# The last stage's normalizing factor: one root per token and a second product, or the root of a broadcast row

## The chip, the cores and the metric

The kernel runs on one core of a Trainium2 chip. A core has five engines with a queue of instructions each: TensorE (PE in the profile) multiplies matrices, with its weight loads shown apart (PEld); VectorE (DVE) and ScalarE (ACT) work elementwise; GpSimd (POOL) works elementwise too, on SBUF alone; SyncE (SP) issues DMAs. They share the memory SBUF, of 128 partitions; products land in a second one, PSUM. The metric is the device time of one execution in microseconds.

## The reference, cut to what matters

One step of a decoder with two layers, for a prompt of 2048 tokens and 8 sample tokens, 1024 wide. The first layer is a Mamba-2 mixer, the second a Conformer convolution module. The change lies in the end of the second:

```
def conformer_conv_mixer(u, conv_buf, w_in, b_in, conv_w, conv_b, ln_g, ln_b, w_out):
    proj = u @ w_in + b_in
    val, glu_gate, z = jnp.split(proj, 3, axis=-1)
    v = val * jax.nn.sigmoid(glu_gate)
    c, new_buf = causal_depthwise_conv(v, conv_buf, conv_w, conv_b)
    c = jax.nn.silu(layer_norm(c, ln_g, ln_b))
    return (c * jax.nn.silu(z)) @ w_out, new_buf
```

`layer_norm` takes, per token, the mean and the variance over 2048 channels and multiplies the centred values by (variance + 1e-6) to the power −1/2. The result of the mixer is normalized once more and added to the layer's input.

## The kernel before

All is float32. A product is made exact enough by splitting its operands into two parts each and adding three products (`wo_hi·hhi`, `wo_hi·hlo`, `wo_lo·hhi` in the profile). Channels lie on the partitions: the 2048 channels of a token are 16 groups of 128, and a tile of the last stage holds 4 groups of 128 tokens, [128, 4, 128].

The kernel goes through the first layer, then projections and convolution of the second (most of VectorE's and GpSimd's work), and then the **last stage**: 17 chunks, 16 of 128 prompt tokens and at the end one of the 8 sample tokens (`ECH`). The order of all work is written out by hand. Each engine does its instructions in the order in which the program issues them, and waits where an operand isn't ready.

A chunk i passes through these steps:

- `e_load` (L1208), `e_gate` (L1225): DMAs of the convolution's output (`cl`, four tiles of four groups) and of the gate (`zl1`).
- `e_sum` (L1243): GpSimd adds the 16 groups together, two additions of 512 columns and a tree of three steps (`tree`, L736). What is left is [128, 128], partial sums per partition.
- `e_mean` (L1253): a product with `onesm`, a 128 × 128 matrix of 1/2048, sums over the partitions and writes each token's mean to all 128 partitions, in PSUM. VectorE subtracts it (L1264, four instructions), ScalarE squares (L1265), GpSimd sums the squares (L1267 and the tree).
- `e_var` (L1271): the sums of squares are the product's stationary operand and one column of `onesm` the moving one, so the variance comes out with the tokens on the partitions, one column. VectorE adds EPS (L1278), GpSimd takes the power −1/2 of that one column (L1279), VectorE scales the rows of the identity by it (L1281, `dg`).
- `e_apply` (L1284): the product of `onesm` with `dg` (L1290) writes each token's factor to all partitions, in PSUM. VectorE multiplies the four tiles by it (L1292).
- `e_act` (L1295): ScalarE takes silu with the layer norm's gain and bias (L1301, four instructions per tile) and of the gate (L1241), VectorE multiplies the two (L1302). `e_split` (L1304) makes the two parts `hhi` (L714, ScalarE) and `hlo` (L720, VectorE) for the output product.
- `out_mm` (L697, L709): 16 steps of 6 matmuls into two PSUM tiles `ps_out`. `e_back1` and `e_back2` (L1359, L1373) normalize, add the input and store.

The main loop (L1384) interleaves four chunks: while the output product of chunk i runs on TensorE, step by step, it issues between the steps

```
    E_VAR, E_SUM, E_APP, E_BACK, E_ACT, E_SPL, E_MEAN = 4, 4, 5, 6, (6, 8, 10, 12), (8, 10, 12, 14), 10
```

that is: `e_back1` of chunk i−1 at step 0; `e_var` of chunk i+1 and then `e_sum` of chunk i+2 at step 4; `e_apply` of i+1 at step 5; `e_back2` of i−1 and the first `e_act` of i+1 at step 6; a quarter of `e_act` and of `e_split` of i+1 at each of steps 8 to 14; `e_mean` of i+2 at step 10. So on GpSimd the `e_sum` of chunk i+2 stands right behind the root of chunk i+1, and on TensorE the mean product of i+2 stands at step 10, behind the variance product of i+1 at step 4. Chunk 0 passes through `e_sum` to `e_split` before the loop, between the last projections (L1315, at `T_MEAN`, `T_VAR`, `T_APP`, `T_ACT`); there ScalarE and VectorE also split the output weights (`wo1.split`), and ScalarE empties the projections' PSUM tiles (`z1_evac`, L1078).

The small products use a ring of two PSUM tiles, `ps_ln`; the output product has four, two chunks' worth. `neghalf` is one column of −0.5.

Of the kernel before, what the change touches and what calls it, by code (L numbers as in the profile page):

```python
# [10 lines left out]
ALU = mybir.AluOpType  # L11
# [4 lines left out]
P = 128  # L16
# [5 lines left out]
INNER = 2048  # L22
# [5 lines left out]
EPS = 1e-6  # L28
# [10 lines left out]
def hybrid_step(ctx: ExitStack, tc: tile.TileContext, I, O):  # L39
    nc = tc.nc  # L40
    V, A, G_, TE, SY = nc.vector, nc.scalar, nc.gpsimd, nc.tensor, nc.sync
# [25 lines left out]
    ident = const.tile([P, P], F32, name="ident")  # L67
    onesm = const.tile([P, P], F32, name="onesm")
    V.memset(onesm, 1.0 / INNER)
    neghalf = const.tile([P, 25], F32, name="neghalf")[:, 0:1]  # L70
# [885 lines left out]
    for i in range(NCH):  # L956
        hl, _, nt, _ = fr[i]
# [236 lines left out]
    oe = Pool("oe", 2, side="right")  # L1194
    pl_ = Pool("ps_ln", 1, PSUM)
# [7 lines left out]
    est = {}  # L1203

    def e_nt(i):
        return S if ECH[i] is None else P
# [64 lines left out]
    def e_var(i):  # L1271
        if i >= NCH:
            return
        nt, t = e_nt(i), est[i].pop()
        pv = pl_.tile([P, 1, P], "ps_ln", bufs=2)
        TE.matmul(pv[:nt, 0, 0:1], t[:, 0, :nt], onesm[:, 0:1], start=True, stop=True)
        s_ = oe.tile([P, 2], "lnsm")
        V.tensor_scalar(s_[:nt, 0:1], pv[:nt, 0, 0:1], EPS, None, ALU.add)  # L1278
        G_.tensor_tensor(s_[:nt, 1:2], s_[:nt, 0:1], neghalf[:nt], ALU.pow)  # L1279
        dg = oe.tile([P, P], "dg", bufs=1)  # L1280
        V.tensor_scalar(dg[:nt, :nt], ident[:nt, :nt], s_[:nt, 1:2], float(INNER), ALU.mult, ALU.mult)  # L1281
        est[i].append(dg)

    def e_apply(i):  # L1284
        if i >= NCH:
            return
        c, dg = est.pop(i)
        nt = e_nt(i)
        pr = pl_.tile([P, 1, P], "ps_ln", bufs=2)
        TE.matmul(pr[:, 0, :nt], onesm[:nt, :], dg[:nt, :nt], start=True, stop=True)  # L1290
        for q in range(4):
            V.tensor_tensor(c[q][:, :, :nt], c[q][:, :, :nt], pr[:, :, :nt].to_broadcast([P, 4, nt]), ALU.mult)  # L1292
        fr[i] = (([], []), nt, c)

    def e_act(i, q):  # L1295
# [19 lines left out]
    for b, i in TAIL:  # L1315
        ps = mm_psum()
        drain(mm_in(ps, wz[i], u1, b))
        z1_evac(tail[i][1], b, ps)
        if (b, i) == (0, 1):
            for q in range(4):  # L1320
                e_gate(0, q)
        if b >= 2 and (b, i) != (4, 1):
            wo1.split(4 * (b - 2) + 2 * (i + 1))
        if (b, i) == T_MEAN:
            e_mean(0)
        if (b, i) == T_VAR:
            e_var(0)
        if (b, i) == T_APP:
            e_apply(0)
        for q in range(4):  # L1330
            if (b, i) == T_ACT[q]:
                e_act(0, q)
                e_gate(1, q)
        if (b, i) == T_SUM1:
            e_sum(1)
        if (b, i) == T_MEAN1:
            e_mean(1)
# [46 lines left out]
    for i in range(NCH):  # L1384
        hl, nt = fr.pop(i)[:2]
        pos = [pe_.tile([P, 512], "ps_out") for _ in range(2)]
        for step, _ in enumerate(out_mm([(*hl, nt, pos)], wo1)):
            if step == 0:
                if prev is not None:
                    mid = e_back1(*prev)  # L1390
            if step == E_VAR:
                e_var(i + 1)
            if step == E_SUM:
                e_sum(i + 2)
            if step == E_APP:
                e_apply(i + 1)
            if step == E_BACK and prev is not None:
                e_back2(prev[0], *mid)
            if step in E_ACT:
                e_act(i + 1, E_ACT.index(step))  # L1400
                e_gate(i + 2, E_ACT.index(step))
            if step in E_SPL:
                e_split(i + 1, E_SPL.index(step))
                e_load(i + 3, [E_SPL.index(step)])
            if step == 6:
                e_res(i)
            if step == E_MEAN:
                e_mean(i + 2)
        prev = (i, pos)
# [84 lines left out]
```

## Time and profile before

| what | us |
|---|---|
| median of 3 runs | 3116.11 (3106.57 to 3118.13) |
| the profiled execution, device time | 3109.03 |
| its span, first to last instruction | 3107.1 |
| TensorE busy | 3018.4 (97% of the span) |
| VectorE busy | 2343.0 (75%) |
| ScalarE busy | 1541.9 (50%) |
| GpSimd busy | 1308.6 (42%) |

The profile is of one execution. Its page gives, for the whole span, each engine's busy time and the costliest groups of instructions; the trace behind it can be asked for a stretch of time, a line or a tile. A row of the timeline gives the start in microseconds from the span's start, the length, the engine, the line of the kernel, the operation and its operands (output<-inputs, partitions × elements); `x3` merges three equal instructions, and a bracket gives the idle time of the engine before the row and what ended it. A row of a group gives, after its count, the busy time in us, the mean of one instruction in ns, and the idle time before them. Matmul records overlap, since a matmul is pipelined behind the one before it; the distance of their starts tells more than their lengths.

### The profile page before, as it was taken

What the parts mean: (1) busy time and instruction counts of PE and PEld (TensorE: products, weight loads), DVE (VectorE), ACT (ScalarE), POOL (GpSimd) and SP (SyncE); (2) the same over time, 40 slices, a digit from 0 to 9 for tenths busy, and PEclk for the clock granted to TensorE, in tenths of its full rate; (3) what the DMA queues carried; (4) which work ended last, traced back from release to release, by engine and by line L of the source; (5) the groups of instructions that cost most, each with busy time, mean ns of one, the idle gap of its engine ahead of it and who ended that gap; (6) DMA issues with size and microseconds to landing.
All of it is one profiled execution on the core that took longest, in us unless ns stands there. A gap on an engine that the chain in (4) does not pass through costs nothing. (4 is left out here: it accounts for less than half of the span.)

```text
span 3107.1 us, 43405 instructions
## 1 busy us (share of the span) xinstructions
PE 3018.4 (97%) x16379; PEld 2544.3 (82%) x16379; DVE 2343.0 (75%) x3234; ACT 1541.9 (50%) x2635; POOL 1308.6 (42%) x1000
## 2 busy tenths in 40 slices
PE   7999999999999999999999999999999999899998
PEld 6788888878878787788878888888888888677776
DVE  6556777678888884545448999999999998566673
ACT  6444434445555544444445554545545545566563
POOL 2112333211111111323325877777868767345551
PEclk9999999999999999999999999999999999999999
DMA  4124444455555556444441121211222124634331
GB/s 154 59 83 126 134 131 134 136 168 186 171 185 172 181 161 220 152 162 170 163 167 49 58 65 50 64 51 54 62 61 62 45 67 130 196 118 143 129 128 56
DMA packets 265537, 373.13 MB, mean 120 GB/s; under 512 B 30904, under 2 KB 187800, under 8 KB 261232
## 3 DMA queue, kind: packets, MB, share of 16 engines
q1 hardware_dynamic: 136080, 280.62, 28.2%
q10 hardware_dynamic: 122656, 67.68, 7.3%
q0 software_dynamic: 6592, 22.05, 1.8%
q8 instruction: 129, 2.11, 0.3%
q14 instruction: 80, 0.66, 0.1%
HBM read 240.47 MB, written 129.82 MB: 119 GB/s over the span
## 5 line engine op out<-in xcount | busy, mean ns | idle before, releaser
L1041 DVE SCALAR_TENSOR_TENSOR ps_acc<-vt,cw,ps_acc 128x1024 f32<-128x1024 f32 x672 | 814.8, 1280 | 6.9 <-ACT ps_acc L1034 5.2
L1047 POOL TENSOR_TENSOR pacc<-pacc,pr 128x1024 f32<-128x1024 f32 x256 | 620.7, 2454 | 111.8 <-ACT pr L1046 109.1
L709 PE MATMUL ps_out<-wo_hi,hhi 128*128 128x512 f32 (+1 forms) x1088 | 433.4, 398 | 9.4 <-ACT hhi L714 9.4
L709 PE MATMUL ps_out<-wo_lo,hhi 128*128 128x512 f32 (+1 forms) x1088 | 426.7, 392 | 0.0
L163 PE MATMUL ps_h<-u_hi,wh 128*128 128x512 f32 (+2 forms) x1920 | 398.6, 350 | 11.1 <-ACT zt L1082 6.6
L709 PE MATMUL ps_out<-wo_hi,hlo 128*128 128x512 f32 x1024 | 401.4, 392 | 0.8 <-DVE hlo L720 0.8
L163 PE MATMUL ps_h<-u_lo,wh 128*128 128x512 f32 (+2 forms) x1920 | 393.5, 347 | 0.0
L163 PE MATMUL ps_h<-u_hi,wl 128*128 128x512 f32 (+2 forms) x1920 | 392.8, 347 | 0.3 <-POOL wl L99 0.3
L163 PEld LDWEIGHTS ps_h<-u_hi,wh 128*128 128x128 f32 x1920 | 317.6, 190 | 59.0 <-ACT zt L1082 7.6
L163 PEld LDWEIGHTS ps_h<-u_lo,wh 128*128 128x128 f32 x1920 | 316.2, 189 | 45.0
L163 PEld LDWEIGHTS ps_h<-u_hi,wl 128*128 128x128 f32 x1920 | 315.5, 189 | 45.4 <-POOL wl L99 0.5
L295 DVE SCALAR_TENSOR_TENSOR acc<-raw,cw,acc 128x512 f32<-128x512 f32 (+1 forms) x360 | 229.0, 644 | 131.8 <-ACT acc L287 71.7
L1046 ACT ACTIVATE pr<-vt,cw 128x1024 f32<-128x1024 f32 x256 | 287.0, 1145 | 67.1 <-POOL pacc L1047 47.4
L99 POOL TENSOR_TENSOR wl<-wraw,wh 128x1024 fp32r<-128x1024 f32 x86 | 214.1, 2489 | 192.9 <-ACT wh L98 190.0
L709 PEld LDWEIGHTS ps_out<-wo_hi,hhi 128*128 128x128 f32 (+1 forms) x1088 | 201.3, 185 | 55.3 <-ACT hhi L714 10.3
L709 PEld LDWEIGHTS ps_out<-wo_lo,hhi 128*128 128x128 f32 (+1 forms) x1088 | 200.9, 185 | 48.2
L709 PEld LDWEIGHTS ps_out<-wo_hi,hlo 128*128 128x128 f32 x1024 | 193.8, 189 | 39.4 <-DVE hlo L720 1.6
L641 POOL DMA_DIRECT2D y_d<-yt x64 | 38.8, 606 | 439.0 <-DVE yt L640 415.9
L163 PE MATMUL ps_mm<-u_hi,wh 128*128 128x512 f32 (+2 forms) x960 | 200.1, 351 | 3.4 <-ACT wh L98 3.4
L163 PE MATMUL ps_mm<-u_lo,wh 128*128 128x512 f32 (+2 forms) x960 | 197.4, 348 | 0.0
L163 PE MATMUL ps_mm<-u_hi,wl 128*128 128x512 f32 (+2 forms) x960 | 197.4, 348 | 0.0
L163 PEld LDWEIGHTS ps_mm<-u_hi,wh 128*128 128x128 f32 x960 | 158.8, 191 | 27.1 <-ACT wh L98 3.9
(308 smaller groups left out, 4868.0 us busy)
## 6 DMA issues: line engine op xcount, KB each, us to landing
rb<-ac_d SPq DMA_DIRECT2D x64, 512.0 KB, 4.3
z_d<-zt ACTq DMA_DIRECT2D x96, 256.0 KB, 2.9
wraw<-w_in SPq DMA_DIRECT2D x48, 512.0 KB, 3.3
xg<-x_d SPq DMA_DIRECT2D x64, 256.0 KB, 3.2
y_d<-yt POOLq DMA_DIRECT2D x64, 256.0 KB, 2.7
wraw_o<-w_out SPq DMA_DIRECT2D x32, 512.0 KB, 4.3
yl<-y_d SPq DMA_DIRECT2D x16, 1024.0 KB, 6.3
zl<-z_d SPq DMA_DIRECT2D x16, 1024.0 KB, 5.5
```

Of the source, the lines that this page charges most:

```text
L99: (eng or G_).tensor_tensor(wl, raw, wh.bitcast(F32), ALU.subtract)
L163: TE.matmul(ps[:, :n], a[:, k, :], x[:, k, o:o + n], start=(j == 0 and k == 0), stop=(j == 2 and k == KD - 1))
L295: V.scalar_tensor_tensor(acc[:, :n], raw[:, k:k + n], cw[:, m, k:k + 1], acc[:, :n], ALU.mult, ALU.add)
L641: G_.dma_start(y_d[c][:, 4 * g:4 * g + 4, :], yt)
L709: TE.matmul(pos[nh][:m], a[q][:, r, :m], w[q][:, r, ns], start=(k == 0 and j == 0), stop=(k == MI - 1 and j == len(parts) - 1))
L1041: V.scalar_tensor_tensor(acc, vt[:, k:k + W], cw1[:, m, k:k + 1], acc, ALU.mult, ALU.add)
L1046: A.activation(pr, vt[:, kk:kk + W], AF.Copy, scale=cw1[:, m, kk:kk + 1])
L1047: G_.tensor_tensor(pacc, pacc, pr, ALU.add)
```

## The change

The variance product now has the operands in the order of the mean product: `onesm` is stationary and the sums of squares move, so the variance of every token is written to all 128 partitions, [128, 128] in PSUM. EPS is added over 128 columns into an SBUF tile `rstd`, GpSimd takes the power −1/2 of its 128 columns in place, and the apply multiplies by that tile, from SBUF. The scaled identity `dg`, the column `lnsm` and the second product go.

```
@@ -1273,23 +1273,19 @@
             return
         nt, t = e_nt(i), est[i].pop()
         pv = pl_.tile([P, 1, P], "ps_ln", bufs=2)
-        TE.matmul(pv[:nt, 0, 0:1], t[:, 0, :nt], onesm[:, 0:1], start=True, stop=True)
-        s_ = oe.tile([P, 2], "lnsm")
-        V.tensor_scalar(s_[:nt, 0:1], pv[:nt, 0, 0:1], EPS, None, ALU.add)
-        G_.tensor_tensor(s_[:nt, 1:2], s_[:nt, 0:1], neghalf[:nt], ALU.pow)
-        dg = oe.tile([P, P], "dg", bufs=1)
-        V.tensor_scalar(dg[:nt, :nt], ident[:nt, :nt], s_[:nt, 1:2], float(INNER), ALU.mult, ALU.mult)
-        est[i].append(dg)
+        TE.matmul(pv[:, 0, :nt], onesm, t[:, 0, :nt], start=True, stop=True)
+        r = oe.tile([P, 1, P], "rstd", bufs=1)
+        V.tensor_scalar(r[:, 0, :nt], pv[:, 0, :nt], EPS, None, ALU.add)
+        G_.tensor_tensor(r[:, 0, :nt], r[:, 0, :nt], neghalf.to_broadcast([P, nt]), ALU.pow)
+        est[i].append(r)
 
     def e_apply(i):
         if i >= NCH:
             return
-        c, dg = est.pop(i)
+        c, r = est.pop(i)
         nt = e_nt(i)
-        pr = pl_.tile([P, 1, P], "ps_ln", bufs=2)
-        TE.matmul(pr[:, 0, :nt], onesm[:nt, :], dg[:nt, :nt], start=True, stop=True)
         for q in range(4):
-            V.tensor_tensor(c[q][:, :, :nt], c[q][:, :, :nt], pr[:, :, :nt].to_broadcast([P, 4, nt]), ALU.mult)
+            V.tensor_tensor(c[q][:, :, :nt], c[q][:, :, :nt], r[:, :, :nt].to_broadcast([P, 4, nt]), ALU.mult)
         fr[i] = (([], []), nt, c)
 
     def e_act(i, q):
```

## The prediction

> **What bounds the kernel now.** I first read the page's slices: TensorE is at 9 in nearly all. The change touches only the last stage, so I looked there: busy time by stretch, one period long.
>
> ```profile
> core 0: us, PE busy (x) PEld busy (x) DVE busy (x) ACT busy (x) POOL busy (x), PEclk, DMA share, GB/s
> 2838.70:2862.30 23.60, 22.81 (x104) 18.66 (x103) 16.23 (x23) 14.22 (x32) 12.16 (x12) 1.00 0.40 134
> ```
>
> One chunk of 128 tokens takes 23.55 us (below), TensorE is busy for all but 0.8 us, and no other engine is full. But a chunk's statistics run round a ring of engines, and the ring must close within one period: variance (e_var), apply, the gating, the next chunk's mean (e_mean), its squares and trees on GpSimd, the next variance. The timeline of one period shows how near it is. The columns are start, length, engine, line, operation; the rows are those that carry the ring.
>
> ```profile
> 2831.26 0.16 DVE L1278 TENSOR_SCALAR lnsm<-ps_ln 128x1 f32<-128x1 f32 x1 [1.81 <-PE ps_ln L1276]
> 2832.08 1.29 DVE L1281 TENSOR_SCALAR dg<-ident,lnsm 128x128 f32<-128x128 f32 x1 [0.66 <-POOL lnsm L1279]
> 2834.01 2.48 DVE L1292 TENSOR_TENSOR cl<-cl,ps_ln 128x512 f32<-128x512 f32 x4 [0.64 <-PE ps_ln L1290]
> 2836.41 1.40 DVE L1378 SCALAR_TENSOR_TENSOR yo<-ps_out,osm,gpost 128x512 f32<-128x512 f32 x2
> 2837.84 1.23 DVE L1379 TENSOR_TENSOR yo<-yo,xr 128x1024 f32<-128x1024 f32 x1
> 2838.99 1.28 DVE L1302 TENSOR_TENSOR cl<-cl,zl 128x512 f32<-128x512 f32 x2
> 2842.43 0.69 DVE L1302 TENSOR_TENSOR cl<-cl,zl 128x512 f32<-128x512 f32 x1 [1.37 <-ACT cl L1301]
> 2843.64 2.47 DVE L1264 TENSOR_TENSOR cl<-cl,ps_ln 128x512 f32<-128x512 f32 x4
> ```
>
> VectorE goes through this list in program order. After the apply (L1292) come the output of the chunk before (L1378, L1379) and the gating, and only then the next chunk's mean subtraction (L1264). GpSimd's rows:
>
> ```profile
> 2831.49 0.55 POOL L1279 TENSOR_TENSOR lnsm<-lnsm,neghalf 128x1 f32<-128x1 f32 x1 [1.14 <-DVE lnsm L1278]
> 2832.01 2.51 POOL L1249 TENSOR_TENSOR tr<-cl 128x512 f32<-128x512 f32 x2
> 2834.60 2.66 POOL L736 TENSOR_TENSOR tr<-tr 128x512 f32<-128x512 f32 x3
> 2846.86 2.40 POOL L1267 TENSOR_TENSOR tr<-tr,tr 128x1024 f32<-128x1024 f32 x1 [9.60 <-ACT tr L1265]
> 2849.34 3.64 POOL L736 TENSOR_TENSOR tr<-tr 128x512 f32<-128x512 f32 x3
> 2855.03 0.55 POOL L1279 TENSOR_TENSOR lnsm<-lnsm,neghalf 128x1 f32<-128x1 f32 x1 [1.13 <-DVE lnsm L1278]
> ```
>
> Root to root is 2855.03 − 2831.49 = 23.54 us, the period. The tree that feeds the variance ends at 2849.34 + 3.64 = 2852.98. TensorE's rows:
>
> ```profile
> 2832.32 0.40 PE L709 MATMUL ps_out<-wo_lo,hhi 128*128 128x512 f32 x1
> 2833.51 0.46 PE L1290 MATMUL ps_ln<-dg,onesm 128*128 128x128 f32 x2 [0.79 <-DVE dg L1281]
> 2834.04 0.40 PE L709 MATMUL ps_out<-wo_hi,hlo 128*128 128x512 f32 x1
> 2840.63 0.39 PE L1258 MATMUL ps_ln<-tr,onesm 128*128 128x128 f32 x2
> 2854.25 0.40 PE L709 MATMUL ps_out<-wo_lo,hhi 128*128 128x512 f32 x1
> 2854.48 0.28 PE L1276 MATMUL ps_ln<-onesm,tr 128*128 128x1 f32 x2
> ```
>
> The variance product starts at 2854.48 in its turn, about 1.3 us after it could have (2852.98 and some 0.2 us of weight load). So TensorE sets the period, and **the ring has only 1.3 us of slack**.
>
> **What the change removes.** TensorE no longer waits for the scaled identity or makes the second product. From 2832.32 to 2834.04 are 1.72 us where two output matmuls need 2 × 0.227 = 0.45 (2854.25 to 2854.48 is one): 1.27 us a chunk. TensorE alone would then run a period of 22.3 us, and 15 chunks would give 19 us. VectorE loses L1281, 1.29 us.
>
> **What it adds.** The variance product has 128 columns for 1, like the mean product (0.39 against 0.28 us). The addition of EPS has 128 columns: at VectorE's rate on PSUM (0.62 us for 512, L1292) some 0.15 us more. Both lie on the ring: 0.2 us. Then two things with a price.
>
> **(a) The root of 128 columns**, P us. The trace has roots of one column only:
>
> ```profile
> L1249 POOL TENSOR_TENSOR tr<-cl 128x512 f32<-128x512 f32 x26 | 32.7, 1277 | 0.0
> L1279 POOL TENSOR_TENSOR lnsm<-lnsm,neghalf 128x1 f32<-128x1 f32 x13 | 7.1, 547 | 17.3 <-DVE lnsm L1278 17.3
> L94 POOL TENSOR_SCALAR osm<-osm 128x1 f32<-128x1 f32 x13 | 2.5, 190 | 1.3
> L1279 POOL TENSOR_TENSOR lnsm<-lnsm,neghalf 8x1 f32<-8x1 f32 x1 | 0.5, 538 | 4.8 <-DVE lnsm L1278 4.8
> ```
>
> A plain one-column instruction takes 190 ns, the root 547: 357 ns are the root's own. They are the same for 8 rows as for 128 (538), so rows run side by side and columns one after the other. An addition of 512 columns costs (1277 − 190) / 511 = 2.1 ns a column. Lower end: all 357 ns are paid once, P = 0.547 + 127 × 0.0021 = 0.8 us. Upper end: all are paid for every column, P = 0.547 + 127 × 0.359 = 46.1 us. The ends are far apart. The nearest row is the root itself, and its 357 ns repeat in every call whatever ran before, which looks like arithmetic and not like a load. A part will be set-up; I take it as large as all that the plain instruction pays, 190 ns, and leave 167 ns a column: an estimate of P = 0.38 + 128 × 0.167 = 21.8 us.
>
> **(b) The apply reads its factor from SBUF** instead of PSUM. What that means beside a busy GpSimd is in these groups (mean ns):
>
> ```profile
> L720 DVE TENSOR_TENSOR hlo<-cl,hhi 128x512 fp32r<-128x512 f32 x51 | 55.3, 1103 | 1.2
> L1264 DVE TENSOR_TENSOR cl<-cl,ps_ln 128x512 f32<-128x512 f32 x52 | 32.1, 679 | 0.0
> 2840.37 0.69 DVE L720 TENSOR_TENSOR hlo<-cl,hhi 128x512 fp32r<-128x512 f32 x1
> 2849.73 2.93 DVE L720 TENSOR_TENSOR hlo<-cl,hhi 128x512 fp32r<-128x512 f32 x2
> ```
>
> L720 reads two SBUF tiles: 0.69 us with GpSimd idle, 2.93 for two while the tree runs, and that tree takes 3.64 us instead of 2.66. L1264, with one operand in PSUM, keeps to 679 ns. L1281 too: its 1.29 us end 0.1 us after the GpSimd addition that began before it. They take turns. Right behind the root GpSimd has e_sum's two additions and three tree steps (2.51 + 2.66 us), and they win the first turn, as they do now over L1281. So the apply waits about 1.25 + 1.25 + 1.25 + 0.75 us for GpSimd's first four, between its own 4 × 0.6: it ends 6.9 us after the root, where now it ends 2836.49 − 2832.04 = 4.45 after it. If it never waited, 0.07 + 2.48 = 2.55.
>
> The Trainium skill, "GPSIMD Engine Reference", Specifications, says that GpSimd's SBUF interfaces are shared with VectorE, in contention where a VectorE instruction has two SBUF inputs; the trace agrees (1103 against 679 ns), and by it the apply is delayed even by a cheap root, while without it 19 us would be gained.
>
> **The sum.** Behind the apply VectorE's order stays: from its end to the end of the tree 2852.98 − 2836.49 = 16.5 us. From the tree to the next root 2855.03 − 2854.48 + 0.2 + 0.25 = 1.0 us, without slack. The ring then takes P + 6.9 + 16.5 + 1.0 = P + 24.4 us, against 22.3 for TensorE: **the ring becomes the bound**. On TensorE the mean product (L1258, now at 2840.63) waits for the e_sum queued behind the root, and after such a wait the clock is down:
>
> ```profile
> 2697.53 0.80 PE L709 MATMUL ps_out<-wo_hi,hhi 128*128 128x512 f32 x1 [7.63 <-ACT hhi L714]
> 2699.46:2703.72 4.26, 4.26 (x11) 3.30 (x10) 4.26 (x4) 1.90 (x3) 2.87 (x3) 0.50 0.36 122
> ```
>
> A granted clock of 0.50 for 4.3 us costs 2.1 us. TensorE's way round (e_sum with the apply's turns 2.51 + 2.66 + 2.4 = 7.6, the product 0.6, 60 matmuls of 0.227 us 13.6, the clock 2.1, in all 23.9) is 0.5 longer than VectorE's 6.9 + 16.5 = 23.4, so with a long P the period is P + 24.9. At 21.8 us: 46.7, 23.15 more than now, and 15 periods hold a root of 128 columns: 347 us. The root of the first chunk lies before them, in the last projections:
>
> ```profile
> 2665.37 0.57 POOL L1279 TENSOR_TENSOR lnsm<-lnsm,neghalf 128x1 f32<-128x1 f32 x1 [5.42 <-DVE lnsm L1278]
> 2671.65 2.47 DVE L1292 TENSOR_TENSOR cl<-cl,ps_ln 128x512 f32<-128x512 f32 x4
> 2686.86 0.69 ACT L1082 ACTIVATE zt<-ps_h,bi 128x512 f32<-128x512 f32 x1 [2.63 <-DMA z_d<-zt]
> ```
>
> Its apply moves from 2671.65 to 2665.5 + 21.8 + 1.3 = 2688.6; ScalarE behind it is nearly full and has 2.6 us to make it up: 14 us. The last root (8 columns of 8 sample tokens) I cost at nothing: its chunk waits little, and only once. No DMA is added; those whose buffers come free later move along. PSUM's ring ps_ln has two users a chunk for three. Forecast: 3109 (the profiled execution's time) + 347 + 14 = **3470 us**. The median of the runs shown lies 7 us higher, 0.2%.
>
> **The rivals.**
> *One column after the other* (forecast): P from 21.8 to 46.1 us. At the upper end 15 × (71.0 − 23.55) + 39 (the first chunk's 41.2 late less 2.6) = 751, so 3860. For it: the 357 ns come in every call. Chance 0.42.
> *Columns overlap*: set-up is most of the 357 ns and columns flow at 15 to 167 ns. P = 2.5 gives 15 × 3.35 = 50, 3159; P = 8 gives 15 × 9.35 = 140, about 3249; up to the forecast. For it: additions flow at 2.1 ns a column, so loops of columns can overlap. Chance 0.34.
> *A cheap root that is still slower*: P = 0.8, the apply kept waiting: 15 × (25.2 − 23.55) = 25, 3134. Chance 0.13. The Trainium skill, "GPSIMD Engine Reference", Elementwise — side-by-side cycle accounting, gives about 2.6 cycles an element, set by the read port, for an instruction with two inputs; taken for the root too, that is an estimate of 0.8 us for it. The additions' 2.1 ns agree with the rule; for a root the traces show one column only.
> *Faster*: the place is the apply. If it doesn't take turns with GpSimd (another order of grants than L720 gets) the ring is P + 2.55 + 16.5 + 1.0 = P + 20.1, and TensorE keeps the bound up to P = 2.2: 3109 − 19 = 3090. It decides at P = 3.5, where the ring is 23.55. Against it: L720's rows. Chance 0.07.
> *Nothing to see*: half the turns and a cheap root, within 15 us. Chance 0.04.
>
> **How the numbers follow.** 0.5% of this kernel is 15.5 us, about what can be told from no change. Slower by more: 0.42 + 0.34 + 0.13 = 0.89; within: 0.04; faster: 0.07. The range goes from the cheap slower case, 3134, to the root at its full price, 3860, and leaves out about 0.11 below and a little above.
>
> **What would show it.** The root's row at L1281's place gives P outright: 21.8 us by the forecast, 0.8 to 46.1 at the ends. The apply's group at 1.2 to 1.7 us each instead of 682 ns shows the turns; at 0.69 it refutes them. The waits of TensorE should name GpSimd's tr at the mean product, and the granted clock in this stage fall below 1.00. The period should be P + 24.4 to P + 24.9. The forecast is wrong where P is far from 21.8; the ring is wrong where the period stays near 23.5 though P is over 4 us.

## The result, and the profile after

The changed kernel takes 3438.51 us in the median of 4 runs (3430.05 to 3439.47), the kernel before 3111.4 (4 runs, 3106.57 to 3118.13): a ratio of 1.1041, with a 95% interval of 1.102 to 1.1062. The profiled execution after took 3439.47 us with a span of 3437.3.

The page after, its slices and the groups that changed most:

```profile
PE   8999999999999999999999999999999555555556
...
POOL 2113333111111032332677876767766577777773
PEclk9999999999999999999999999999999877777778
...
L1279 POOL TENSOR_TENSOR rstd<-rstd,neghalf 128x128 f32<-128x128 f32 (+1 forms) x17 | 333.4, 19611 | 20.2 <-DVE rstd L1278 20.0
L1288 DVE TENSOR_TENSOR cl<-cl,rstd 128x512 f32<-128x512 f32 x64 | 96.0, 1557 | 328.8 <-POOL rstd L1279 328.8
...
L1258 PE MATMUL ps_ln<-tr,onesm 128*128 128x128 f32 (+1 forms) x34 | 13.0, 484 | 305.4 <-POOL tr L736 305.4
```

In the last nine slices TensorE fell from 9 to 5 and its clock to 7. The time went into three rows that are one: the root is 333 us of GpSimd, VectorE stood 329 us before the apply for it, and TensorE 305 us before the mean product, whose sums stand behind the root in GpSimd's queue.

One period, GpSimd's rows of the timeline after:

```profile
2823.79 20.73 POOL L1279 TENSOR_TENSOR rstd<-rstd,neghalf 128x128 f32<-128x128 f32 x1
2844.49 2.92 POOL L1249 TENSOR_TENSOR tr<-cl 128x512 f32<-128x512 f32 x2
2847.50 3.59 POOL L736 TENSOR_TENSOR tr<-tr 128x512 f32<-128x512 f32 x3
2861.15 2.40 POOL L1267 TENSOR_TENSOR tr<-tr,tr 128x1024 f32<-128x1024 f32 x1 [10.05 <-ACT tr L1265]
2863.62 3.64 POOL L736 TENSOR_TENSOR tr<-tr 128x512 f32<-128x512 f32 x3
...
2868.21 20.73 POOL L1279 TENSOR_TENSOR rstd<-rstd,neghalf 128x128 f32<-128x128 f32 x1
```

and VectorE's apply and TensorE's two products:

```profile
2844.55 6.22 DVE L1288 TENSOR_TENSOR cl<-cl,rstd 128x512 f32<-128x512 f32 x4 [20.84 <-POOL rstd L1279]
```

```profile
2851.14 0.80 PE L1258 MATMUL ps_ln<-tr,onesm 128*128 128x128 f32 x2 [19.55 <-POOL tr L736]
...
2867.32 0.49 PE L1276 MATMUL ps_ln<-tr,onesm 128*128 128x128 f32 x2
```

The ring can be read off. The root ends at 2823.79 + 20.73 = 2844.52; the apply at 2844.55 + 6.22 = 2850.77, 6.25 after it; the tree at 2863.62 + 3.64 = 2867.26, 16.49 after the apply; the next root starts 0.95 later. 20.73 + 6.25 + 16.49 + 0.95 = 44.42 us, the distance of the two roots. The apply's instructions take 1557 ns in the mean where they took 682, and the sums beside them 2.92 + 3.59 us where they took 2.51 + 2.66: the turns of the two engines, paid on both. VectorE's four starts are 1.67 us apart, where the prediction had 1.25 + 0.6 = 1.85 for a turn.

TensorE's clock, the last number but two of these rows (busy time by stretch, over the period and over the 4.18 us that follow the mean product's wait):

```profile
2823.79:2868.21 44.42, 24.76 (x102) 19.80 (x101) 18.76 (x21) 14.21 (x32) 33.70 (x12) 0.77 0.22 71
```

```profile
2851.14:2855.32 4.18, 4.17 (x11) 3.40 (x12) 4.05 (x6) 1.33 (x3) 0.00 (x0) 0.50 0.28 109
```

It is granted 0.77 of full speed in the mean and 0.50 in the 4.18 us after work resumes, where the period before had 1.00.

The roots of chunks 1 and 15 mark the ends of 14 periods. Before:

```profile
2712.27 0.55 POOL L1279 TENSOR_TENSOR lnsm<-lnsm,neghalf 128x1 f32<-128x1 f32 x1 [9.78 <-DVE lnsm L1278]
...
3043.43 0.55 POOL L1279 TENSOR_TENSOR lnsm<-lnsm,neghalf 128x1 f32<-128x1 f32 x1 [1.13 <-DVE lnsm L1278]
```

After, with the root of chunk 0 ahead of them:

```profile
2673.24 20.78 POOL L1279 TENSOR_TENSOR rstd<-rstd,neghalf 128x128 f32<-128x128 f32 x1 [6.02 <-DVE rstd L1278]
...
2735.49 20.74 POOL L1279 TENSOR_TENSOR rstd<-rstd,neghalf 128x128 f32<-128x128 f32 x1 [9.50 <-DVE rstd L1278]
...
3356.91 20.73 POOL L1279 TENSOR_TENSOR rstd<-rstd,neghalf 128x128 f32<-128x128 f32 x1
```

| stretch | before, us | after, us | difference |
|---|---|---|---|
| start to root of chunk 0 | 2665.37 | 2673.24 | +7.9 |
| root of chunk 0 to root of chunk 1 | 46.90 | 62.25 | +15.3 |
| 14 periods, root of chunk 1 to root of chunk 15 | 331.16 | 621.42 | +290.3 |
| root of chunk 15 to the end | 63.67 | 80.39 | +16.7 |
| span | 3107.1 | 3437.3 | +330.2 |

The first 7.9 us lie ahead of every changed instruction, except the one product and addition that feed that root. Executions of the kernel before alone spread over some 20 us (3101.67 to 3122.53 in the runs below), so these 7.9 us aren't charged to the change.

### The profile page after: what moved, and what is told of

Same layout as the page of the kernel before. It is cut to its first block, busy times and chain, and to the rows that moved or that the text cites. A ratio compares the mean times of both kernels' runs of the same rounds, so it can differ in the third digit from the quotient of the medians.

```text
span 3437.3 us, 43302 instructions
## 1 busy us (share of the span) xinstructions
PE 3045.0 (89%) x16345; PEld 2560.2 (74%) x16345; DVE 2391.3 (70%) x3217; ACT 1543.0 (45%) x2635; POOL 1652.7 (48%) x1000
## 5 line engine op out<-in xcount | busy, mean ns | idle before, releaser
L709 PE MATMUL ps_out<-wo_hi,hhi 128*128 128x512 f32 (+1 forms) x1088 | 442.1, 406 | 14.1 <-ACT hhi L714 14.1
L709 PE MATMUL ps_out<-wo_hi,hlo 128*128 128x512 f32 x1024 | 409.3, 400 | 0.8 <-DVE hlo L720 0.8
L1279 POOL TENSOR_TENSOR rstd<-rstd,neghalf 128x128 f32<-128x128 f32 (+1 forms) x17 | 333.4, 19611 | 20.2 <-DVE rstd L1278 20.0
L1288 DVE TENSOR_TENSOR cl<-cl,rstd 128x512 f32<-128x512 f32 x64 | 96.0, 1557 | 328.8 <-POOL rstd L1279 328.8
L1258 PE MATMUL ps_ln<-tr,onesm 128*128 128x128 f32 (+1 forms) x34 | 13.0, 484 | 305.4 <-POOL tr L736 305.4
L1297 ACT ACTIVATE cl<-cl,lnb,lng 128x128 f32<-128x128 f32 x256 | 104.8, 480 | 381.4 <-DVE cl L1288 381.4
L1258 PEld LDWEIGHTS ps_ln<-tr,onesm 128*128 128x128 f32 x34 | 8.3, 304 | 312.3 <-POOL tr L736 312.3
```

Source lines behind the costliest of these rows:

```text
L709: TE.matmul(pos[nh][:m], a[q][:, r, :m], w[q][:, r, ns], start=(k == 0 and j == 0), stop=(k == MI - 1 and j == len(parts) - 1))
L1279: G_.tensor_tensor(r[:, 0, :nt], r[:, 0, :nt], neghalf.to_broadcast([P, nt]), ALU.pow)
L1288: V.tensor_tensor(c[q][:, :, :nt], c[q][:, :, :nt], r[:, :, :nt].to_broadcast([P, 4, nt]), ALU.mult)
L1297: A.activation(c[q][:, k - 4 * q, :nt], c[q][:, k - 4 * q, :nt], AF.Silu, bias=lnb[:, k:k + 1], scale=lng[:, k:k + 1])
```

## The experiments

The theory, after the result: the ring on VectorE's side sets the period at root + 23.7 us, of which the turns at the apply are 3.7 (6.25 for 2.55); the root costs 0.37 us once and 0.159 us a column. The last comes from the rows above and the sample chunk's root, this group after:

```profile
L1279 POOL TENSOR_TENSOR rstd<-rstd,neghalf 128x8 f32<-128x8 f32 x1 | 1.6, 1644 | 2.7 <-DVE rstd L1278 2.7
```

(20.73 − 1.644) / 120 = 0.159 us a column. The rivals are that TensorE's low clock sets the period, that the turns cost nothing and only the root does, and that the root's price isn't one of columns.

### The root without its price

In the changed kernel:

```
-        G_.tensor_tensor(r[:, 0, :nt], r[:, 0, :nt], neghalf.to_broadcast([P, nt]), ALU.pow)
+        G_.tensor_tensor(r[:, 0, :nt], r[:, 0, :nt], neghalf.to_broadcast([P, nt]), ALU.mult)
```

> The changed kernel with a plain multiplication of 128 columns by -0.5 where the root was (the factor, and so the output, is another). Theory (the ring of statistics is root + 23.7 us: 6.25 to the end of the apply, which takes turns with GpSimd, 16.5 from there to the end of the tree, 0.95 to the next root): about 0.46 us for the multiplication, a period of 24.15 us against 23.55 before, 15 x 0.6 = 9 us slower than before, about 3118 us, and still slower though the root is free; apply instructions of 1.2 to 1.7 us. Rival (only the root's price made the change slow, the apply's turns cost nothing): TensorE keeps the bound at 22.3 us a period, about 3090 us.

Measured: 3114.17 us (11 runs) against 3112.93 for before, ratio 1.0009 (0.9994 to 1.0023). GpSimd's rows of this run:

```profile
2760.23 0.40 POOL L1279 TENSOR_TENSOR rstd<-rstd,neghalf 128x128 f32<-128x128 f32 x1
...
2784.40 0.40 POOL L1279 TENSOR_TENSOR rstd<-rstd,neghalf 128x128 f32<-128x128 f32 x1
```

and VectorE's:

```profile
2784.84 6.30 DVE L1288 TENSOR_TENSOR cl<-cl,rstd 128x512 f32<-128x512 f32 x4 [0.51 <-POOL rstd L1279]
```

The period is 24.17 us, forecast 24.15: with the root at 0.40 us and the second product gone, the ring is still longer than the 23.55 of before. The apply takes 6.3 us again, so the turns don't come from a long root. The whole time doesn't show the 9 us: the interval reaches from 2 us faster to 7 us slower. In the profiled executions the thirteen middle periods of the loop are 7.3 us longer together, and the two ahead of them and the one behind are 3.0 us shorter, which the forecast hadn't counted. The turns also vary: in one of the thirteen periods VectorE waited once only and got the other three instructions through in a row, and the apply ended 3.64 us after the root. The interval excludes the 19 us of gain that the rival gives, so a cheap root alone would not have made the change pay.

### The same, with the factor in PSUM

Beside the multiplication, the apply reads a copy:

```
         nt = e_nt(i)
+        pr = pl_.tile([P, 1, P], "ps_ln", bufs=2)
+        A.activation(pr[:, 0, :nt], r[:, 0, :nt], AF.Copy)
         for q in range(4):
-            V.tensor_tensor(c[q][:, :, :nt], c[q][:, :, :nt], r[:, :, :nt].to_broadcast([P, 4, nt]), ALU.mult)
+            V.tensor_tensor(c[q][:, :, :nt], c[q][:, :, :nt], pr[:, :, :nt].to_broadcast([P, 4, nt]), ALU.mult)
```

> As the run with the multiplication, and ScalarE copies the factor into PSUM, where the apply reads it as it did before the change. Theory: without the root's price and without turns the ring is about 20.8 us, TensorE bounds at 22.3 us a period, 15 x 1.25 = 19 us faster than before, about 3090 us; apply instructions of 0.68 us. Rival (the second product's wait was worth nothing, since the ring or another wait takes its place): within 5 us of before, 3104 to 3114 us.

Measured: 3083.07 us (5 runs), ratio 0.9917 (0.9901 to 0.9933). The roots' places and the apply:

```profile
2773.74 0.40 POOL L1279 TENSOR_TENSOR rstd<-rstd,neghalf 128x128 f32<-128x128 f32 x1 [0.93 <-DVE rstd L1278]
...
2795.98 0.40 POOL L1279 TENSOR_TENSOR rstd<-rstd,neghalf 128x128 f32<-128x128 f32 x1 [0.95 <-DVE rstd L1278]
```

```profile
L1290 DVE TENSOR_TENSOR cl<-cl,ps_ln 128x512 f32<-128x512 f32 x60 | 37.2, 681 | 12.4 <-ACT ps_ln L1288 12.4
```

22.24 us a period, forecast 22.3: TensorE's own, which is busy for the whole of it. Between the two profiled executions the whole fell by 26 us; 20.5 of them lie between the first root and the last, for the 19 expected, and the rest lies outside, within the spread of executions, some 10 us for this kernel. So both steps of the prediction stand apart: the second product and its wait were worth 1.3 us a chunk, and the turns are what takes them away when the root is cheap.

### A root of 32 columns

```
-        G_.tensor_tensor(r[:, 0, :nt], r[:, 0, :nt], neghalf.to_broadcast([P, nt]), ALU.pow)
+        G_.tensor_tensor(r[:, 0, :min(nt, 32)], r[:, 0, :min(nt, 32)], neghalf.to_broadcast([P, min(nt, 32)]), ALU.pow)
```

> The changed kernel with the root taken of 32 of the 128 columns (the other tokens keep their variance as factor). Theory (0.37 us once and 0.159 us a column, the ring on VectorE's side root + 23.7): root 5.5 us, period 29.15 us, 15 x 5.6 = 84 us over before, about 3193 us. Rival 1 (TensorE's way round with its low clock sets the period, root + 24.9): period 30.4, about 3211 us. Rival 2 (the price is that of a wide root, not of its columns): near 3438 us.

Measured: 3189.42 us, ratio 1.0247 (1.0229 to 1.0266). GpSimd's groups in the last stage of this run:

```profile
L1279 POOL TENSOR_TENSOR rstd<-rstd,neghalf 128x32 f32<-128x32 f32 x13 | 70.5, 5423 | 1.9 <-DVE rstd L1278 1.7
L1279 POOL TENSOR_TENSOR rstd<-rstd,neghalf 128x8 f32<-128x8 f32 x1 | 1.6, 1642 | 0.9 <-DVE rstd L1278 0.9
```

The root takes 5.42 us for a forecast 5.5, and the whole is within 4 us of the theory's 3193. Of the loop's thirteen middle periods nine lie within 0.05 us of the forecast 29.15. The other four are longer, up to 29.76: in these the low clock lasted longest, 5.3 to 6.2 us behind the mean product's wait, and TensorE's way round closed the ring, so Rival 1 holds in part, at a fraction of its price. 8, 32 and 128 columns (1.64, 5.42, 20.73 us) lie on one line: columns don't overlap.

### The root at its price, the factor in PSUM

The changed kernel with the copy into PSUM alone.

> The changed kernel with its root of 128 columns, and ScalarE copies the factor into PSUM for the apply. Theory: the apply no longer takes turns and ends 2.9 us after the root instead of 6.25; VectorE's side of the ring shortens by 3.3 us, but TensorE's side (root, 5.2 us of sums and trees now undisturbed, 16.0 us from the mean product to the variance product) is then the longer: period about 42.8 us for 44.4, 15 x 1.6 = 25 us less than the changed kernel, about 3413 us; by VectorE's side alone it would be 3385. Rival (the apply is slow because both operands are in SBUF, turns or not, and costs the ring nothing): within 5 us of the changed kernel, 3433 to 3443 us.

Measured: 3430.88 us, ratio 1.1024 (1.0987 to 1.1061). Neither figure: nearer the rival's. The timeline of this run shows why, first VectorE and GpSimd, then TensorE:

```profile
2884.31 2.48 DVE L1290 TENSOR_TENSOR cl<-cl,ps_ln 128x512 f32<-128x512 f32 x4 [21.16 <-ACT ps_ln L1288]
```

```profile
2863.23 20.73 POOL L1279 TENSOR_TENSOR rstd<-rstd,neghalf 128x128 f32<-128x128 f32 x1 [2.72 <-DVE rstd L1278]
2883.94 2.50 POOL L1249 TENSOR_TENSOR tr<-cl 128x512 f32<-128x512 f32 x2
2886.51 3.47 POOL L736 TENSOR_TENSOR tr<-tr 128x512 f32<-128x512 f32 x3
...
2907.54 20.73 POOL L1279 TENSOR_TENSOR rstd<-rstd,neghalf 128x128 f32<-128x128 f32 x1 [2.77 <-DVE rstd L1278]
```

```profile
2845.77 0.80 PE L1258 MATMUL ps_ln<-tr,onesm 128*128 128x128 f32 x2 [19.04 <-POOL tr L736]
...
2862.44 0.39 PE L1276 MATMUL ps_ln<-tr,onesm 128*128 128x128 f32 x2
```

The apply did leave the turns: it ends at 2886.79, 2.83 us after the root's end (2883.96) where it ended 6.25 after. But the period is 44.31 us, 0.1 less than the change's. TensorE now closes the ring: the sums end 6.02 us after the root, from the mean product to the variance product are 16.67, from there to the root 0.79; with the root 44.2. I had put 5.2 and 16.0 for the first two. The sums now take turns with VectorE's next instructions on two SBUF tiles (L1377 takes 1.52 us, where the same addition, L1379, took 1.23 in the kernel before). And the low clock lasts longer than in the changed kernel, 5.69 us behind the mean product's wait where it was 4.18:

```profile
2845.77:2851.46 5.69, 5.69 (x14) 4.56 (x15) 4.23 (x8) 3.72 (x8) 0.00 (x0) 0.50 0.84 275
```

So the rival's time came nearly true, but not for its reason: the apply's gain is lost on TensorE's side.

### Two runs that tell the sides apart

The mean product one step later moves it on TensorE alone: VectorE has nothing in step 11. Once on top of the factor in PSUM, once in the changed kernel:

```
-    E_VAR, E_SUM, E_APP, E_BACK, E_ACT, E_SPL, E_MEAN = 4, 4, 5, 6, (6, 8, 10, 12), (8, 10, 12, 14), 10
+    E_VAR, E_SUM, E_APP, E_BACK, E_ACT, E_SPL, E_MEAN = 4, 4, 5, 6, (6, 8, 10, 12), (8, 10, 12, 14), 11
```

> As the run with the factor in PSUM (root of 128 columns, 3431 us), with the mean product at step 11 instead of 10, which changes TensorE's order alone: no VectorE instruction is issued in step 11. Theory (there TensorE's side of the ring sets the period: after the mean product 60 matmuls follow up to the variance product, 16.7 us with the low clock): 54 matmuls are left, 1.4 us less a period, 15 x 1.4 = 21 us less, about 3410 us. Rival (the gain of that run was lost in another place than TensorE's side): 3426 to 3436 us as in that run.

> The changed kernel (apply from SBUF) with the mean product at step 11. Theory (here VectorE's side sets the period, TensorE's is a few tenths of a us shorter): no change, 3433 to 3443 us. Rival (TensorE's side with its low clock sets the period in the changed kernel too, as the prediction had it): 21 us less, about 3417 us.

Measured, with the factor in PSUM: 3398.65 us, ratio 1.0927 (1.0906 to 1.0949), where it was 1.1024. GpSimd's roots:

```profile
2844.75 20.73 POOL L1279 TENSOR_TENSOR rstd<-rstd,neghalf 128x128 f32<-128x128 f32 x1 [0.44 <-DVE rstd L1278]
...
2887.84 20.73 POOL L1279 TENSOR_TENSOR rstd<-rstd,neghalf 128x128 f32<-128x128 f32 x1 [1.56 <-DVE rstd L1278]
...
2929.92 20.73 POOL L1279 TENSOR_TENSOR rstd<-rstd,neghalf 128x128 f32<-128x128 f32 x1 [0.55 <-DVE rstd L1278]
```

Periods of 43.09 and 42.08 us for 44.31: TensorE's order alone shortens them, so it set them. The gain, 32 us between the two medians, is more than the 21 expected. The rest is the clock's, as the first stretch behind the mean product's wait shows in these two periods:

```profile
2871.55:2877.70 6.15, 6.15 (x16) 4.89 (x17) 4.69 (x8) 4.18 (x9) 0.00 (x0) 0.50 0.88 289
...
2914.64:2918.66 4.02, 4.02 (x11) 3.25 (x12) 2.56 (x5) 3.21 (x7) 0.00 (x0) 0.50 0.83 244
```

The low clock lasts 2.1 us less in the second; at half speed that is 1.07 us of work, and the period is 1.01 shorter. Over the 14 periods between chunks 1 and 15 it lasts 4.5 us in the mean, for 5.9 in the run before, which makes 0.7 us a period; with the 1.4 us of six matmuls some 2 us were to be expected, and the mean period went from 44.29 to 42.33.

Measured in the changed kernel: 3432.65 us, ratio 1.1032 (1.1011 to 1.1053), which includes the change's 1.1041. Two roots and TensorE's waits in the loop:

```profile
2864.39 20.73 POOL L1279 TENSOR_TENSOR rstd<-rstd,neghalf 128x128 f32<-128x128 f32 x1
...
2908.80 20.73 POOL L1279 TENSOR_TENSOR rstd<-rstd,neghalf 128x128 f32<-128x128 f32 x1
```

```profile
PE ps_ln L1276 <- POOL tr L736: 11.4, 13, 1.0
```

44.41 us, as without it; TensorE only waits longer for the tree at the variance product (11.4 us in 13 waits, for 2.7 us in 10 waits in the changed kernel). In the changed kernel VectorE's side is the bound, and TensorE's follows closely.

### The wide root in the kernel before

```
         dg = oe.tile([P, P], "dg", bufs=1)
+        G_.tensor_tensor(dg[:nt], s_[:nt, 0:1].to_broadcast([nt, P]), neghalf[:nt].to_broadcast([nt, P]), ALU.pow)
         G_.tensor_tensor(s_[:nt, 1:2], s_[:nt, 0:1], neghalf[:nt], ALU.pow)
```

The wide root is written into `dg`, which the scaled identity overwrites. A form in which `lnsm` was widened to hold the 128 roots did not fit into SBUF, and there is no time of it.

> The kernel before, with a root of 128 equal columns put in front of its root of one column; its result is not used. Scaled identity, second product and apply from PSUM as before. Theory: GpSimd is busy 21.3 us more or less as in the changed kernel, but TensorE stands at the second product until root and identity are done and then has its steps 5 to 16 and 0 to 4 still to do, about 24.4 us: period about 46.5 us, 15 x 22.9 + 13 = 357 us over before, about 3466 us, more than the changed kernel. Rival (VectorE's side sets the period, root + 4.45 + 16.5 + 0.8 = 43.0 us): about 3414 us, less than the changed kernel.

Measured: 3490.44 us, ratio 1.1221 (1.1202 to 1.124). GpSimd's roots of three chunks and of the last:

```profile
2825.88 20.74 POOL L1280 TENSOR_TENSOR dg<-lnsm,neghalf 128x128 f32<-128x128 f32 x1 [2.21 <-DVE lnsm L1278]
...
2872.52 20.74 POOL L1280 TENSOR_TENSOR dg<-lnsm,neghalf 128x128 f32<-128x128 f32 x1 [3.23 <-DVE lnsm L1278]
...
2918.12 20.74 POOL L1280 TENSOR_TENSOR dg<-lnsm,neghalf 128x128 f32<-128x128 f32 x1 [2.20 <-DVE lnsm L1278]
```

```profile
3425.04 20.73 POOL L1280 TENSOR_TENSOR dg<-lnsm,neghalf 8x128 f32<-8x128 f32 x1 [5.36 <-DVE lnsm L1278]
```

TensorE's rows:

```profile
2848.58 0.77 PE L1291 MATMUL ps_ln<-dg,onesm 128*128 128x128 f32 x2 [21.48 <-DVE dg L1282]
...
2858.11 0.39 PE L1258 MATMUL ps_ln<-tr,onesm 128*128 128x128 f32 x2
...
2871.96 0.28 PE L1276 MATMUL ps_ln<-onesm,tr 128*128 128x1 f32 x2
```

Periods of 46.64 and 45.60 us in turn, forecast 46.5, and not VectorE's 43.0: TensorE waits 21.48 us at the second product and has its steps still to do. What exceeds the expected 3466 us is mostly one root: I had left out that the sample chunk's would be 128 columns wide too, 20.73 us on its 8 rows. Less that root and the 16 one-column roots that this kernel does on top (0.54 us each), 3490 − 20.7 − 8.6 = 3461 us are left, still above the change's 3438.5: with a root at this price the change's structure is the better of the two, and the wide root accounts for more than the whole loss. The rows also give the clock's price: the mean product to the variance product takes 13.85 us here, where TensorE comes to it at speed, 16.67 with the factor in PSUM, where it comes from a wait and has the low clock for 5.69 us, and 16.18 in the changed kernel, with 4.18 us of low clock and a short wait at the end.

### The identity scaled on ScalarE

In the kernel before:

```
-        V.tensor_scalar(s_[:nt, 0:1], pv[:nt, 0, 0:1], EPS, None, ALU.add)
+        V.tensor_scalar(s_[:nt, 0:1], pv[:nt, 0, 0:1], EPS, 1.0 / INNER / INNER, ALU.add, ALU.mult)
...
-        V.tensor_scalar(dg[:nt, :nt], ident[:nt, :nt], s_[:nt, 1:2], float(INNER), ALU.mult, ALU.mult)
+        A.activation(dg[:nt, :nt], ident[:nt, :nt], AF.Copy, scale=s_[:nt, 1:2])
```

> The kernel before, with the identity scaled on ScalarE instead of VectorE (the factor 2048 goes into the addition of EPS). Theory: of the 1.27 us that TensorE loses per chunk at the second product, some 0.85 us are VectorE waiting its turn with GpSimd; ScalarE takes no turns, so TensorE's period falls to about 22.7 us, 15 x 0.85 = 13 us faster than before, about 3096 us. Rival (ScalarE comes too late or the wait is the second product's own): within 5 us of before.

Measured: 3100.0 us (7 runs), ratio 0.9954 (0.9936 to 0.9971). Roots and TensorE's rows round the second product:

```profile
2776.33 0.55 POOL L1279 TENSOR_TENSOR lnsm<-lnsm,neghalf 128x1 f32<-128x1 f32 x1 [0.90 <-DVE lnsm L1278]
...
2798.96 0.55 POOL L1279 TENSOR_TENSOR lnsm<-lnsm,neghalf 128x1 f32<-128x1 f32 x1 [0.91 <-DVE lnsm L1278]
```

```profile
2777.16 0.40 PE L709 MATMUL ps_out<-wo_lo,hhi 128*128 128x512 f32 x1
2777.39 0.47 PE L1290 MATMUL ps_ln<-dg,onesm 128*128 128x128 f32 x2
2777.61 0.48 PE L709 MATMUL ps_out<-wo_hi,hhi 128*128 128x512 f32 x1
```

```profile
2776.91 0.41 ACT L1281 ACTIVATE dg<-ident,lnsm 128x128 f32<-128x128 f32 x1 [3.70 <-POOL lnsm L1279]
```

The scaling takes 0.41 us on ScalarE, beside GpSimd's sums, for 1.29 on VectorE. The period is 22.63 us, forecast 22.7: TensorE no longer waits before the second product. It is the kernel before with one scaling on another engine, and faster than either of the two.

## Why the prediction was right

It said 3470 us in a range of 3134 to 3860; it was 3438.51.

**The ring becomes the bound.** Right: the period is root + 23.7 us, forecast root + 24.4 to 24.9. The 16.5 and 1.0 us of its second part were measured as 16.49 and 0.95.

**The root of 128 columns.** 20.73 us for 21.8. The choice between 0.8 and 46.1 was a guess at how much of the one-column root is paid once: I took 380 ns and 167 a column, the runs show 370 and 159. That it came so near is partly luck; the row of one column could not say it. The rival of overlapping columns is refuted by the straight line through 8, 32 and 128.

**The turns.** Right in kind, and 6.25 us for 6.9: each of the first three took 1.67 us for 1.85, and the last 1.21 for 1.35.

**TensorE's way round, 0.5 us longer through its low clock.** Wrong: in the changed kernel VectorE's side is the longer, shown by the mean product moved one step without effect. The term that was too large is the sums: from the root's end to the mean product TensorE waits 6.62 us (2851.14 − 2844.52), not 7.6. From there to the variance product it takes 16.18 us for 16.3, the last tenths of them waiting for the tree. The low clock lasted 4.18 us where 4.3 were counted, and so cost the 2.1 us of the forecast. That this fits is luck: the row it came from begins at 2699.46, but TensorE had resumed work at 2697.53, so the low clock lasted some 6.2 us there. In the periods of these runs it lasts between 2.8 and 6.2 us, and with the factor in PSUM it cost 2.8 us (16.67 less 13.85). The Trainium skill, "TensorE: Matmul & The Clock Gate", Part 1, says that an idle array runs at half clock and gets the full one after some 3.4 us of work. The rows agree on the half clock, with 0.50 in the stretch behind the wait; on the length they do not always, with 4.18 us in the changed kernel and 5.69 with the factor in PSUM.

The period was so forecast at 46.7 us for 44.42: 1.07 less in the root, 0.65 in the turns, and 0.5 because TensorE's way round is not the longer one. By the table 14 periods add 290.3 us where 14 × 23.15 = 324.1 were forecast, 34 less, and the last chunk adds 16.7 for 23, 6 less; the first adds 15.3 for 14, and the head of the span 7.9 that aren't the change's. Together that is 31 us less than forecast, the distance of 3470 and the profiled 3439.

**The rival on the faster side** would have needed an apply without turns. The copy into PSUM gives that, and with a cheap root the 19 us are there (22.24 us a period). Once the turns are gone the root's price decides, and GpSimd's root of 128 columns is 20.73 us, not 0.8.

## What to carry to other kernels

A stage in which TensorE is busy 97% can still hold a ring through the other engines with little slack; before a change to one of its links, add up the whole ring and compare it with the period. An elementwise operation that shows one duration at one width tells nothing of its price per column: measure two widths. And where an operand moves from PSUM to SBUF, look at what GpSimd does at that moment: VectorE's instructions with two operands, both in SBUF, mostly waited in these runs for the GpSimd instruction under way to end.

## What the runs showed of the hardware

GpSimd's power costs 0.37 us and 0.159 us a column, and the same 20.73 us for 128 columns on 8 rows as on 128. A multiplication of the same 128 columns costs 0.40 us, a fiftieth. The turns between the two engines slow both: GpSimd's sums went from 5.17 to 6.51 us while VectorE's four multiplications went from 2.48 to 6.22. In one of thirteen periods with the cheap root the turns fell out otherwise, and three of the four came through in a row. TensorE's clock after a wait was 0.50 for a length that differs from one period to the next, 2.8 to 6.2 us in these runs.
